# An attention block's output product: sums of weight blocks and the residual made by transfers in DRAM, a fixed order, and three of seven products one after another

## The chip, the cores and the metric

One core of one Trainium2 chip runs one program. The metric is the device time of one execution in microseconds. TensorE (PE in the rows) does the matrix products, VectorE (DVE) and ScalarE (ACT) the elementwise work, GpSimd (POOL) a few masks and casts. Transfers are issued from the queue of SyncE (SP) and from that of GpSimd; 16 DMA engines carry them all.

## The reference

With 512 tokens of width 4096 the reference computes one attention layer and a last RMSNorm:

```python
h = rms_norm(x, norm_g)
proj = h @ w_in + b_in                          # 4096 x 9216: q 4096, k 512, v 512, z 4096
q, k, v, z = jnp.split(proj, [...], axis=-1)
# 64 query heads of 64, 8 key heads; window of 128 keys; one sink a head
p = e / (jnp.sum(e, axis=-1, keepdims=True) + jnp.exp(sink - m))
o = jnp.einsum('bnkgqs,bnskd->bnqkgd', p, vv)
x = x + (o * jax.nn.silu(z)) @ w_out + b_out    # 4096 x 4096
return rms_norm(x, final_g)
```

All is float32. The kernel keeps that precision by splitting each operand of a product into a rounded half "hi" and the rest "lo", and by three TensorE passes for each block: hi·hi, hi·lo, lo·hi.

## The kernel before

**First part, until about 1744 us.** The value columns are multiplied first, then 68 tiles of 128 columns of `w_in` (a key tile for every two key groups, four q tiles and four z tiles for each of eight groups). A tile takes eight chunks (`kc`) of 12 products. SyncE loads `raw` (512 KB, two chunks); ScalarE rounds it to `whi`, VectorE subtracts to `wlo`. The steps of the attention are put between the chunks by a clock of chunks (`at`, `tick`): `scores`, then `turn` (transpose, round, and up to four GpSimd masks, L464), two ticks later `attend`. When the four query blocks of a head pair and its gate are there, `finish` multiplies them and GpSimd's queue stores the head pair to `gT` in DRAM (L550). TensorE's instructions keep program order (`mm`, `tr`); the order on the other engines comes from a scheduler.

**Second part, the output product, from there to the end.** Left operand (the gated heads, transposed) and `w_out` are cut into 2 x 2 blocks, and seven products M1 to M7 of sums of blocks (Strassen) take the place of eight. Each has four column chunks (`p`) of 512, each chunk eight steps (`j`), each step 12 matmuls for two row blocks. They run in three stages. `chunk_35` does M3 and M5 side by side, `chunk_167` M1, M6 and M7, `chunk_42` M4 and M2. A step of `chunk_167` loads four blocks of `w_out`, GpSimd's queue adds a fifth to one of them in SBUF by an accumulating transfer (L771), and VectorE adds two pairs (L681). Then each right operand is rounded by ScalarE (L146) and subtracted by VectorE (L147) into a ring of four slots (`RING`). The left operands are loaded from `gT` as stages, added by VectorE, and split the same way (`left_35`, `left_167`, `left_42`). The residual `x` is loaded into the four output tiles `y` early in `chunk_35` (`begin`, 1 MB each) and `b_out` is added there by accumulating transfers.

At the end of each chunk the accumulators are added into `y` all together:

```python
    for i in range(2):
        a, b = y_of(i, p * CW, CW), y_of(2 + i, D // 2 + p * CW, CW)
        add(a, m1[i], a)
        add(b, m1[i], b)
```

The left operands of the first three quarters of M3 and M5 are made while the last tile of the first part runs (`FIRST`). The last chunk of `chunk_42` scales the rows and stores them.

Of the kernel before, what the change touches and what calls it, by code (L numbers as in the profile page):

```python
# [35 lines left out]
LATE = NP // 2  # L36
EPS = 1e-5
# [5 lines left out]
LAST = 3  # L43

# [7 lines left out]
def hybrid_block_kernel(  # L52
# [20 lines left out]
    ps_m = ctx.enter_context(tc.tile_pool(name="ps_m", bufs=4, space=PS))  # L73
    wpool = ctx.enter_context(tc.tile_pool(name="wpool", bufs=1))
    xg = ctx.enter_context(tc.tile_pool(name="xg", bufs=1))
    small = ctx.enter_context(tc.tile_pool(name="small", bufs=1))
# [57 lines left out]
    gT = dram.tile([KT, P, S], F32, name="gT")  # L134
    def block_of(u, v, j):

        kt = (v * NQ + j) * KC
        return gT[kt:kt + KC, :, u * HALF:(u + 1) * HALF].rearrange("k p s -> p k s")
# [40 lines left out]


    def left(n, src):

        t = slot(n, [P, 2, KC, HALF], "left")
        split(src, t[:, 0], t[:, 1])
        return t

    def fetch_blocks(t, *blocks):
        for i, b in enumerate(blocks):
            nc.sync.dma_start(t[:, i], block_of(*b))

    L35 = {}
    staged = {}

    def stage_35(j):
        staged[j] = slot(j % 2, [P, 2, KC, HALF], "stage", F32)
        fetch_blocks(staged[j], (0, 0, j), (0, 1, j))

    def left_35(j):

        t = staged[j]  # L200
        a = left(L_35[j][0], t[:, 0])
        nc.vector.tensor_tensor(t[:, 0], t[:, 0], t[:, 1], op=ALU.add)
        L35[j] = a, left(L_35[j][1], t[:, 0])

    L_35 = ((2, 3), (4, 5), (8, 9), (10, 11))
    RING = (6, 7, 12, 13)
    FIRST = {
        0: lambda: behind(lambda: (stage_35(0), stage_35(1))),
        2: lambda: behind(lambda: left_35(0)),
        3: lambda: behind(lambda: left_35(1)),  # L210
        4: lambda: behind(lambda: stage_35(2)),
        5: lambda: behind(lambda: left_35(2)),
    }


    with ExitStack() as ph:
        att = ph.enter_context(tc.tile_pool(name="att", bufs=1))
# [4 lines left out]
        def split_w(raw, j, copy=nc.scalar.copy):  # L222
            hi = att.tile([P, CW], F32R, name="whi", tag="whi", bufs=WB)
            lo = att.tile([P, CW], F32R, name="wlo", tag="wlo", bufs=WB)
# [323 lines left out]
        def finish(g, p, o, z):  # L548
            nc.vector.tensor_tensor(o, o, z, op=ALU.mult)
            nc.gpsimd.dma_start(gT[g * 4 + p], o)  # L550
# [93 lines left out]
        while due:  # L644
            tick()
# [332 lines left out]
```

## Time and profile before

| what | value |
|---|---|
| time before, median of 3 runs | 2556.26 us (2554.64 to 2563.33) |
| the profiled execution: its time / its span | 2559.72 us / 2557.9 us |
| TensorE busy | 2395.6 us, 94% of the span |
| VectorE busy | 1541.1 us, 60% |
| ScalarE busy | 950.7 us, 37% |
| GpSimd busy | 313.0 us, 12% |
| mean DMA rate | 150 GB/s |
| mean granted clock of TensorE | 0.973 |

The span is the time from the first to the last instruction of the profiled execution; all stretches below are counted from its start. TensorE's busy time includes matmuls that run slowly or overlap, so a busy TensorE isn't a TensorE at its best pace; how many matmuls a stretch holds tells more.

### The profile page before, as it was taken

The numbers are of one execution on the slowest core, as the hardware profiler recorded it, in microseconds if no ns is written. First come the engines' busy times: TensorE is split into PE (matmuls) and PEld (weight loads), VectorE is DVE, ScalarE is ACT, GpSimd is POOL, SyncE is SP. The second block draws the span as 40 slices with busy tenths as digits, with TensorE's granted clock in tenths as the row PEclk, the third lists the DMA queues.
The fourth block names the chain that finished last, engine by engine and source line by source line (L and its number), as shares of the span: only waits on it lengthen the run. The fifth ranks groups of instructions, "written<-read, shape, count | busy, mean of one in ns | idle before, by whom it ended". The sixth has DMA issues, their size and how long they took to land.

```text
span 2557.9 us, 29388 instructions
## 1 busy us (share of the span) xinstructions
PE 2395.6 (94%) x10604; PEld 1945.4 (76%) x10604; DVE 1541.1 (60%) x2462; ACT 950.7 (37%) x1867; POOL 313.0 (12%) x454
## 2 busy tenths in 40 slices
PE   9999999999999999999999999995699788888986
PEld 7888888888888888888888888874477566666765
DVE  5445655646556555565464655664768666576667
ACT  6433433424333333343333343341334322233434
POOL 1101211201021021021020111111000000000000
PEclk9999999999999999999999999997899999999998
DMA  9523332233232232332333323336777988898555
GB/s 336 177 91 94 90 103 92 90 111 91 91 105 90 88 108 88 99 97 91 99 93 99 99 83 105 97 122 207 248 240 238 284 245 244 242 300 273 181 166 213
DMA packets 119315, 384.24 MB, mean 150 GB/s; under 512 B 12992, under 2 KB 29376, under 8 KB 117376
## 3 DMA queue, kind: packets, MB, share of 16 engines
q1 hardware_dynamic: 104032, 329.37, 39.0%
q0 software_dynamic: 14992, 52.70, 8.6%
q8 instruction: 84, 1.38, 0.2%
q14 instruction: 63, 0.52, 0.1%
q10 hardware_dynamic: 144, 0.28, 0.0%
HBM read 361.32 MB, written 20.97 MB: 149 GB/s over the span
## 4 chain that ended last, share of the span: by engine, by line
PE 70%; DMA 16%; DVE 9%; issue 4%; ACT 1%; SPq 0%; POOL 0%; DVEq 0%; ACTq 0%; POOLq 0%
PE acc L115 65%; DMA raw<-in_w_out 13%; DVE right L147 3%; DMA stage<-gT 2%; DVE raw L681 2%; PE ps L115 2%; PE po L115 2%; DVE y L681 1%; PE pt L118 1%; DMA y<-in_x 1%; ACT right L146 0%; DVE left L147 0%; DMA yd<-st 0%; DVE stage L681 0%; DVE st L681 0%
## 5 line engine op out<-in xcount | busy, mean ns | idle before, releaser
L115 PE MATMUL acc<-xhi,whi 128*128 128x512 f32 x2176 | 863.3, 397 | 0.0
L115 PE MATMUL acc<-xhi,wlo 128*128 128x512 f32 x2176 | 861.0, 396 | 0.0
L115 PE MATMUL acc<-xlo,whi 128*128 128x512 f32 x2176 | 860.7, 396 | 0.0
L115 PE MATMUL acc<-right,left 128*128 128x512 f32 x2688 | 663.4, 406 | 133.2 <-ACT right L146 67.6
L115 PEld LDWEIGHTS acc<-right,left 128*128 128x128 f32 x2688 | 520.5, 196 | 275.8 <-DVE right L147 87.6
L147 DVE TENSOR_TENSOR wlo<-raw,whi 128x512 fp32r<-128x512 f32 x576 | 402.9, 700 | 527.6 <-ACT whi L146 518.3
L146 ACT CAST whi<-raw 128x512 fp32r<-128x512 f32 x575 | 357.0, 621 | 880.6 <-PE acc L115 833.9
L115 PEld LDWEIGHTS acc<-xhi,wlo 128*128 128x128 f32 x2176 | 411.3, 189 | 94.7
L115 PEld LDWEIGHTS acc<-xhi,whi 128*128 128x128 f32 x2176 | 411.8, 189 | 87.9
L115 PEld LDWEIGHTS acc<-xlo,whi 128*128 128x128 f32 x2176 | 411.4, 189 | 88.0
L146 ACT CAST right<-raw 128x1024 fp32r<-128x1024 f32 x224 | 230.1, 1047 | 435.9 <-DMA raw<-in_w_out 223.0
L147 DVE TENSOR_TENSOR right<-raw,right 128x1024 fp32r<-128x1024 f32 x224 | 268.4, 1218 | 71.9 <-ACT right L146 71.5
L681 DVE TENSOR_TENSOR raw<-raw 128x1024 f32<-128x1024 f32 x128 | 156.2, 1222 | 176.8 <-DMA raw<-in_w_out 169.0
L464 POOL TENSOR_SCALAR_AFFINE_SELECT ww<-wh 64x512 fp32r<-64x512 f32 x64 | 42.5, 664 | 913.6 <-ACT wh L460 913.6
L536 DVE RECIPROCAL e<-e 128x128 f32<-128x128 f32 x128 | 120.4, 942 | 0.4
L438 ACT ACTIVATE prob<-ps,nm 128x128 f32<-128x128 f32 x256 | 90.4, 365 | 74.2 <-DVE nm L429 73.2
L513 ACT COPY ot<-po 64x256 f32<-64x256 f32 x128 | 46.9, 366 | 66.5 <-DVE o L514 39.7
L771 POOL DMA_DIRECT2D raw<-in_w_out x32 | 27.5, 859 | 318.8 <-DVE raw L681 172.1
L514 DVE TENSOR_TENSOR o<-po,ot 64x256 f32<-64x256 f32 x128 | 52.8, 412 | 20.9 <-ACT ot L513 20.3
L313 DVE TENSOR_TENSOR tmp<-acc,rbc 128x512 f32<-128x512 f32 x37 | 25.6, 692 | 66.0 <-PE acc L115 66.0
L387 DVE SCALAR_TENSOR_TENSOR q<-tmp,bcol,q 64x512 fp32r<-64x512 f32 x64 | 58.7, 917 | 7.3 <-ACT q L386 6.3
L447 DVE TENSOR_SCALAR prob<-prob,den 128x128 f32<-128x128 f32 x256 | 56.0, 282 | 2.2
(130 smaller groups left out, 1606.5 us busy)
## 6 DMA issues: line engine op xcount, KB each, us to landing
raw<-in_w_in SPq DMA_DIRECT2D x272, 512.0 KB, 3.6
raw<-in_w_out SPq DMA_DIRECT2D x256, 512.0 KB, 5.5
stage<-gT SPq DMA_DIRECT2D x32, 512.0 KB, 6.5
raw<-in_w_out POOLq DMA_DIRECT2D x32, 512.0 KB, 8.7
row<-in_x POOLq DMA_DIRECT2D x16, 512.0 KB, 6.0
gT<-o POOLq DMA_DIRECT2D x32, 256.0 KB, 2.3
xraw<-in_xT SPq DMA_DIRECT2D x15, 512.0 KB, 6.7
raw<-in_w_v SPq DMA_DIRECT2D x15, 512.0 KB, 6.2
```

Of the source, the lines that this page charges most:

```text
L115: tc.keep_in_program_order(nc.tensor.matmul(*a, **k))
L146: copy(hi, src),
L147: nc.vector.tensor_tensor(lo, src, hi.bitcast(F32), op=ALU.subtract),
L387: nc.vector.scalar_tensor_tensor(q2[other, :, h, :], tv[own], b[own], q2[own, :, h, :].bitcast(F32), op0=ALU.add, op1=ALU.subtract,)
L438: nc.scalar.activation(pr[:, u, a, :], ps[:, u, a, 0:P], AF.Exp, bias=nm[:, u, a:a + 1], scale=SCALE, accum_out=den[:, u, a:a + 1],)
L447: nc.vector.tensor_scalar_mul(pr[:, u, a, :], pr[:, u, a, :], den[:, u, a:a + 1])
L464: nc.gpsimd.affine_select(out=out, in_=src.bitcast(F32), fill=0.0, pattern=[[0, 8], [1 if own else -1, QH]], compare_op=ALU.is_ge if own e ...
L513: nc.scalar.copy(ot[own], pq[other, :, :, h, :])
L514: nc.vector.tensor_tensor(ov[own], pq[own, :, :, h, :], ot[own], op=ALU.add)
L536: nc.vector.reciprocal(c, c)
L681: nc.vector.tensor_tensor(out, a, b, op=op)
L771: nc.gpsimd.dma_start(r21, part_w(1, 1, p, j), accum_op=ALU.add)
```

## The change

It has five parts.

1. **Sums of `w_out` in DRAM.** `sums_in_dram` lists 96 pairs of blocks (the right operands of M1, M6 and M7) and 32 pieces of `x` with `b_out`. `make_sums`, called at every second chunk of the first part, issues from GpSimd's queue either a copy of one block into DRAM or, four copies later, a transfer that adds the second block to it there. Each is made to wait for ScalarE's rounding of the weight chunk at hand.
2. **Sums of left blocks in DRAM.** `keep_g` stores each head pair to `gT` in another layout, and by three more transfers into `left_sum` (for M5, M1 and M2); for the later half of the heads those three accumulate.
3. **One product at a time.** `chunk_167` becomes `chunk_single`, called for M1, M6 and M7 in turn: a step loads one sum, splits it and runs 12 matmuls.
4. **Fixed order.** In the second part SyncE's loads, ScalarE's and VectorE's work keep program order (`q`, `ordered`), except in the last chunk. What is to be done at a chunk's end is put in a queue (`later`), and a step of the next chunk takes one item of it (`some`).
5. **Residual.** `y` is first written by copies of the accumulators, and the pieces of `xb` are added to it by accumulating transfers, or loaded where they are first needed. The SBUF pools are laid out anew (`small` first, `halves` apart).

The diff, cut to its core:

```diff
+    gT = dram.tile([2, 2 * NQ, P, KC, HALF], F32, name="gT")
+    left_sum = {m: dram.tile([NQ, P, KC, HALF], F32, name=f"left{m}") for m in (5, 1, 2)}
+    right_sum = {m: dram.tile([NH2, NP, P, 2 * CW], F32, name=f"right{m}") for m in (1, 6, 7)}
+    xb = dram.tile([NB, P, D], F32, name="xb")
+
+    def part_w(u, v, p, j):
+
+        return w_out[NH2 * v + p, NP * u + j]
+
+    def sums_in_dram():
+        for p in range(NH2):
+            for j in range(NP):
+                for m, a, b in ((1, (0, 0), (1, 1)), (6, (0, 0), (0, 1)), (7, (1, 0), (1, 1))):
+                    yield right_sum[m][p, j], part_w(*a, p, j), part_w(*b, p, j)
+            for c in range(2):
+                cs = slice((2 * p + c) * CW, (2 * p + c + 1) * CW)
+                for tb in range(NB):
+                    yield xb[tb][:, cs], x[tb * P:(tb + 1) * P, cs], b_out[:, cs].broadcast_to([P, CW])
+
+    def keep_g(g, p, o):
+
+        nc.gpsimd.dma_start(
+            gT[:, g, :, p].rearrange("u q s -> q u s"), o.rearrange("q (u s) -> q u s", u=2)
+        )
+        late = g >= NQ
+        for m, u in ((5, 0), (1, int(late)), (2, 1)):
+            out, half = left_sum[m][g % NQ][:, p], o[:, u * HALF:(u + 1) * HALF]
+            if late:
+                nc.gpsimd.dma_start(out, half, accum_op=ALU.add)
+            else:
+                nc.gpsimd.dma_start(out, half)
...
+    def right_35(p, j):
+        r12, r22 = raw_w(part_w(0, 1, p, j)), raw_w(part_w(1, 1, p, j))
+        add(r12, r12, r22, ALU.subtract)
+        w5 = right(r22)
+        return right(r12), w5
...
+        def make_sums():
+            do = next(sums_to_do, None) if len(begun) < AHEAD else None
+            if do:
+                out_, a, b = do
+                begun.append((out_, b))
+                turn_ = nc.gpsimd.dma_start(out_, a, max_dma_last_dim=4 * CW)
+            elif begun:
+                out_, b = begun.pop(0)
+                turn_ = nc.gpsimd.dma_start(out_, b, accum_op=ALU.add, max_dma_last_dim=4 * CW)
+            else:
+                return
+
+            tc.add_manual_dep(
+                turn_.ins, latest[1].ins.name,
+                mybir.DependencyInfo(mybir.DependencyClass.Sync, mybir.DependencyReason.DATA),
+                reason="pace",
+            )
...
-                if t == NT - 1 and kc in FIRST:
-                    FIRST[kc]()
+                if t == NT - 1 and kc == 0:
+                    behind(lambda: (stage_35(0), stage_35(1)))
+                if t == NT - 1 and kc == 2:
+                    behind(lambda: left_35(0))
+                if t == NT - 1 and kc == NC - 1:
+                    behind(lambda: first.append(right_35(0, 0)))
+                if t and kc % 2:
+                    make_sums()
...
+    def left_of(m, j, n):
+        if m == 1 or m == 2:
+            t = staging(left_sum[m][j])
+        elif m == 4:
+            t = staging(gT[1, NQ + j])
+        else:
+            v = 0 if m == 6 else NQ
+            t, b = (staging(gT[u, v + j]) for u in ((1, 0) if m == 6 else (0, 1)))
+            add(t, t, b, ALU.subtract)
+        L[m, j] = left(n, t)
...
+    def some():
+        if queue:
+            queue.pop(0)()
...
+        def land(i):
+            a, b = chunk_of(i, p), chunk_of(2 + i, NH2 + p)
+            q(nc.scalar.copy(b, m3[i]))
+            q(nc.scalar.mul(a, m5[i], -1.0))
+            add(sts[i], m3[i], sts[i])
+            add(sts[i], m5[i], sts[i])
+            residual(a, i, p, accum_op=ALU.add)
+            residual(b, 2 + i, NH2 + p, accum_op=ALU.add)
...
+    def chunk_single(m, p, between):
+        acc = accumulator()
         for j in range(NP):
+            w = right(raw_w(right_sum[m][p, j]))
+            if j in between:
+                between[j]()
+            if j > 2:
+                some()
+            mm_pair(acc, m, j, w)
...
-            r11, r22, r12, r21 = (raw_w(u, v, p, j) for u, v in ((0, 0), (1, 1), (0, 1), (1, 0)))
-            nc.gpsimd.dma_start(r21, part_w(1, 1, p, j), accum_op=ALU.add)
-            add(r22, r22, r11)
-            w1 = right(r22)
-            add(r12, r12, r11)
-            w6, w7 = right(r12), right(r21)
...
+    ordered[0] = True
+
+    for p in range(NH2):
+        between = {
+            0: {0: lambda: left_35(1), 2: lambda: (stage_35(2), left_35(2)),
+                4: lambda: (stage_35(3), left_35(3))},
+            1: {k: lambda k=k: left_of(1, k // 2, (14, 15, 0, 1)[k // 2]) for k in (0, 2, 4, 6)},
+        }
+        chunk_35(p, between.get(p, {}))
+    for p in range(NH2):
+        chunk_single(1, p, {
+            1: lambda: left_of(6, p, (2, 3, 4, 5)[p]),
+            5: lambda: left_of(7, p, (8, 9, 10, 11)[p]),
+        })
+    for p in range(NH2):
+        chunk_single(6, p, {1: lambda: left_of(4, p, (14, 15, 0, 1)[p])} if p < 2 else {})
+    for p in range(NH2):
+        chunk_single(7, p, {
+            1: lambda: left_of(2, p, (2, 3, 4, 5)[p]),
+            5: lambda: left_of(4, p, (14, 15, 0, 1)[p]) if p > 1 else None,
+        })
+    for i in range(2):
+        for n, (tb, h) in ((8 + i, (i, 1)), (10 + i, (2 + i, 0))):
+            y[tb, h] = slot(n, [P, D // 2], f"y{tb}{h}", F32)
+    for p in range(NH2):
         chunk_42(p)
```

**Where instructions move: GpSimd in the first part.** Below, its rows after the third `turn` of a head quad, before the change; `qq` is a cast for the next quad, `gT` the store of a head pair.

```order
L464 AFFINE_SELECT ww<-wh 64x512
L464 AFFINE_SELECT ww<-wl 64x512
L464 AFFINE_SELECT wh<-wh 64x512
L464 AFFINE_SELECT wl<-wl 64x512
L550 DMA gT<-o 128x512 x2
L397 CAST qq<-q_1969 64x8x64 x2
```

And the rows there after it; `right_94` and `right_95` are the sums for M6 and M7, `left_90` to `left_92` those for M5, M1 and M2. L621 is a copy, L624 an accumulate.

```order
L524 AFFINE_SELECT ww<-wh 64x512
L524 AFFINE_SELECT ww<-wl 64x512
L524 AFFINE_SELECT wh<-wh 64x512
L524 AFFINE_SELECT wl<-wl 64x512
L621 DMA right_94<-in_w_out 256x512
L164 DMA gT<-o 128x2x256
L173 DMA left_90<-o 128x256
L173 DMA left_91<-o 128x256
L173 DMA left_92<-o 128x256
L624 DMA right_94<-in_w_out 256x512
L621 DMA right_95<-in_w_out 256x512
```

Transfers for the sums now stand before and after the masks, and each store of a head pair has become four.

**VectorE in the last tile of the first part.** Before, ahead of `prob`, the row that TensorE's last transposes wait for:

```order
L539 SCALAR_TENSOR_TENSOR z<-z,bcol,e 128x512
L514 TENSOR_TENSOR o<-po,ot 64x2x2x64
L147 TENSOR_TENSOR left<-stage,left 128x1024
L433 TENSOR_TENSOR es<-nm,sink 128x4
L514 TENSOR_TENSOR o<-po,ot 64x2x2x64
L147 TENSOR_TENSOR left<-stage,left 128x1024
L443 TENSOR_TENSOR den<-den,es 128x4
L202 TENSOR_TENSOR stage<-stage 128x1024
L444 RECIPROCAL den<-den 128x4
L681 TENSOR_TENSOR raw<-raw 128x1024
L447 TENSOR_SCALAR prob<-prob,den 128x128 x4
```

The same place after it:

```order
L599 SCALAR_TENSOR_TENSOR z<-z,bcol,e 128x512
L239 TENSOR_TENSOR right<-raw,right 128x1024
L574 TENSOR_TENSOR o<-po,ot 64x2x2x64
L493 TENSOR_TENSOR es<-nm,sink 128x4
L574 TENSOR_TENSOR o<-po,ot 64x2x2x64
L503 TENSOR_TENSOR den<-den,es 128x4
L504 RECIPROCAL den<-den 128x4
L507 TENSOR_SCALAR prob<-prob,den 128x128 x4
```

The left operands of the second and third quarter, their additions and one weight addition no longer stand there.

**SyncE's queue at the start of the second part.** Before (`y_14618` to `y_14627` are the four output tiles):

```order
L668 DMA raw<-in_w_out 128x1024 x2
L700 DMA y_14618<-in_x 128x2048
L700 DMA y_14621<-in_x 128x2048
L700 DMA y_14624<-in_x 128x2048
L700 DMA y_14627<-in_x 128x2048
L700 DMA st<-in_x 128x512 x2
L755 DMA stage<-gT 128x4x256
L668 DMA raw<-in_w_out 128x1024
```

After:

```order
L228 DMA raw<-in_w_out 128x1024 x5
L228 DMA stage<-gT 128x1024
L228 DMA stage<-left_90 128x1024
L228 DMA raw<-in_w_out 128x1024 x4
L228 DMA stage<-gT 128x1024
L228 DMA stage<-left_90 128x1024
L228 DMA raw<-in_w_out 128x1024 x4
L228 DMA st<-xb 128x512 x2
```

The four 1 MB loads of `x` are gone from between the weights; only weights, stages and two pieces of `xb` follow one another.

## Rows read from the trace of the kernel before

**Rows 1.** By stretch: us, busy (count) PE PEld DVE ACT POOL, clock, DMA share, GB/s.
```profile
100.00:1700.00 1600.00, 1600.00 (x7365) 1320.40 (x7364) 911.67 (x1749) 591.42 (x1402) 237.44 (x341) 1.00 0.31 97
...
1744.00:1811.00 67.00, 25.55 (x99) 19.64 (x98) 27.01 (x29) 13.82 (x15) 7.34 (x10) 0.70 0.88 269
1811.00:1960.00 149.00, 138.16 (x586) 110.48 (x586) 112.64 (x115) 58.69 (x65) 10.32 (x15) 0.99 0.69 224
1960.00:2312.00 352.00, 293.38 (x1156) 225.46 (x1154) 228.93 (x214) 108.90 (x111) 28.36 (x34) 0.94 0.88 264
2312.00:2500.00 188.00, 167.91 (x696) 133.57 (x696) 132.59 (x139) 72.89 (x93) 4.79 (x7) 0.95 0.64 203
```

**Rows 2.** Busy time in a stretch with few stalls.
```profile
1900.00:1950.00 50.00, 47.22 (x206) 38.13 (x205) 36.09 (x37) 20.84 (x24) 4.55 (x7) 1.00 0.68 221
```

**Rows 3.** The groups of the output product's instructions by line.
```profile
L115 PE MATMUL acc<-right,left 128*128 128x512 f32 x2688 | 663.4, 406 | 133.2 <-ACT right L146 67.6 <-DVE right L147 63.1 <-DVE sq L852 2.2
...
L147 DVE TENSOR_TENSOR right<-raw,right 128x1024 fp32r<-128x1024 f32 x224 | 268.4, 1218 | 71.9 <-ACT right L146 71.5
L146 ACT CAST right<-raw 128x1024 fp32r<-128x1024 f32 x224 | 230.1, 1047 | 435.9 <-DMA raw<-in_w_out 223.0 <-PE acc L115 139.7 <-DVE raw L681 70.1
L681 DVE TENSOR_TENSOR raw<-raw 128x1024 f32<-128x1024 f32 x128 | 156.2, 1222 | 176.8 <-DMA raw<-in_w_out 169.0 <-issue 7.4
```

**Rows 4.** TensorE's waits from 1960 to 2312 us: total, times, longest.
```profile
PE acc L115 <- DVE right L147: 38.2, 32, 4.5
PE acc L115 <- ACT right L146: 20.2, 13, 4.3
```

**Rows 5.** DMA queues from 1960 to 2312 us: packets, MB, share of 16 engines.
```profile
q1 hardware_dynamic: 25423, 75.51, 60.8%
q0 software_dynamic: 4824, 17.09, 26.6%
```

**Rows 6.** TensorE's timeline at the start of the second part: start, us, instruction.
```profile
1743.87 5.65 PE L115 MATMUL acc<-right,left 128*128 128x512 f32 x24
...
1763.59 18.16 PE L115 MATMUL acc<-right,left 128*128 128x512 f32 x71 [1.65 <-DVE right L147]
1808.43 0.80 PE L115 MATMUL acc<-right,left 128*128 128x512 f32 x1 [26.69 <-ACT right L146]
```

**Rows 7.** GpSimd's and SyncE's timelines there.
```profile
1751.68 0.55 POOL L550 DMA_DIRECT2D gT<-o  x1 [0.83 <-DVE o L549]
...
1754.33 0.34 SPq L668 DMA_DIRECT2D raw<-in_w_out  x1
...
1756.35 2.29 SPq L700 DMA_DIRECT2D y<-in_x  x4
```

**Rows 8.** VectorE's groups from 1700 to 1744 us.
```profile
L147 DVE TENSOR_TENSOR left<-stage,left 128x1024 fp32r<-128x1024 f32 x7 | 8.4, 1213 | 2.8 <-ACT left L146 2.8
L202 DVE TENSOR_TENSOR stage<-stage 128x1024 f32<-128x1024 f32 x3 | 3.8, 1256 | 0.0
```

**Rows 9.** The tail: TensorE's last row in its timeline.
```profile
2502.16 38.23 PE L115 MATMUL acc<-right,left 128*128 128x512 f32 x155 [2.98 <-DVE right L147]
```

**Rows 10.** DMA from 100 to 1700 us: two queues, and a weight load's time to landing.
```profile
q1 hardware_dynamic: 38705, 140.96, 28.6%
q0 software_dynamic: 4015, 12.51, 2.3%
...
raw<-in_w_in SPq DMA_DIRECT2D x267, 512.0 KB, 3.6
```

**Rows 11.** GpSimd's issues by line.
```profile
L771 POOL DMA_DIRECT2D raw<-in_w_out x32 | 27.5, 859 | 318.8 <-DVE raw L681 172.1 <-DMA raw<-in_w_out 73.2 <-DVE y L681 22.5
...
L550 POOL DMA_DIRECT2D gT<-o x32 | 17.6, 550 | 179.9 <-DVE o L549 179.9
```

**Rows 12.** A head block's last mask and the product that needs it, in the timeline.
```profile
1307.44 1.17 POOL L464 TENSOR_SCALAR_AFFINE_SELECT wl<-wl 64x512 fp32r<-64x512 f32 x1
...
1308.95 0.28 PE L115 MATMUL po<-wh,vv 128*128 128x256 f32 x1
```

More of the change, by code (lines that the diff above doesn't have):

```diff
@@ L177, in load_w, with q, take @@
         return raw
-    def left(n, src):
[L183 to L191, printed above, removed]
+    ordered = [False]
+    def q(ins):
+        return tc.keep_in_program_order(ins) if ordered[0] else ins
+    RING = (6, 7, 12, 13)
+    count = {"raw": 0, "acc": 0, "w": 0}
+    def take(name):
+        count[name] += 1
+        return count[name] - 1
@@ new lines, in load, with raw_w, divide, right @@
+    def load(t, src):
+        q(nc.sync.dma_start(t, src))
+    def raw_w(src):
+        pool = outp if take("raw") // RAW % 2 else wpool
+        raw = pool.tile([P, 2, CW], F32, name="raw", tag="raw", bufs=RAW)
+        load(raw, src.rearrange("p (j c) -> p j c", j=2))
+        return raw
+    def divide(src, t):
+        q(nc.scalar.copy(t[:, 0], src))
+        q(nc.vector.tensor_tensor(t[:, 1], src, t[:, 0].bitcast(F32), op=ALU.subtract))
+        return t
+    def right(raw, place=None):
+        t = slot(RING[take("w") % 4] if place is None else place, [P, 2, 2, CW], "right")
+        return divide(raw, t)
@@ L192, in hybrid_block_kernel, with add @@
+    def left(n, src):
+        return divide(src, slot(n, [P, 2, KC, HALF], "left"))
+    def add(out, a, b, op=ALU.add):
+        q(nc.vector.tensor_tensor(out, a, b, op=op))
+    def right_35(p, j):
[3 more added lines that the diff above has]
+        return right(r12), w5
+    first = []
+    L = {}
     staged = {}
     def stage_35(j):
-        staged[j] = slot(j % 2, [P, 2, KC, HALF], "stage", F32)
@@ L196, in stage_35 @@
-        fetch_blocks(staged[j], (0, 0, j), (0, 1, j))
+        staged[j] = t = slot(j % 2, [P, 2, KC, HALF], "stage", F32)
+        load(t[:, 0], gT[0, j])
+        load(t[:, 1], left_sum[5][j])
     def left_35(j):
[L200 to L213, printed above, removed]
+        n = ((2, 3), (4, 5), (8, 9), (10, 11))[j]
@@ L643, in hybrid_block_kernel @@
                 evacuate(g_, name, acc)
+        assert not begun and next(sums_to_do, None) is None
         while due:
@@ L691, in mm_pair, with mm_block @@
-    def mm_pair(acc, j, lt, rt):
-        for i in range(2):
-            mm_block(acc[i], i, j, lt, rt)
+            (ps_m, ps_n)[take("acc") // 4 % 2].tile([P, CW], F32, name="acc") for _ in range(2)
+        ]
+    def mm_block(acc, i, m, j, rt):
+        for k in range(2):
+            l = L[m, j // 2][:, :, (2 * j + k) % KC, i * P:(i + 1) * P]
+            mm(acc[i], l[:, 0], rt[:, 0, k], start=(j == k == 0), stop=False)
+            mm(acc[i], l[:, 0], rt[:, 1, k], start=False, stop=False)
+            mm(acc[i], l[:, 1], rt[:, 0, k], start=False, stop=(j == NP - 1 and k == 1))
@@ L703, in gains_of, with chunk_of, residual @@
+    def chunk_of(tb, cc):
+        return y_of(tb, cc * CW, CW)
+    def residual(t, tb, cc, **k):
+        src = xb[tb][:, cc * CW:(cc + 1) * CW]
+        if k:
+            nc.gpsimd.dma_start(t, src, **k)
+        else:
+            load(t, src)
     def gains_of(cc):
@@ L811, in chunk_42 @@
             w4 = right(r21)
-            late = last and j >= LATE
-            w2 = right(r11, (S_42[0] + S_42[1])[j - LATE] if late else None)
-            mm_pair(m4, j, L42[j // 2][0], w4)
+            if j > 1:
+                some()
+            if j == (1 if last else NP - 2):
+                fgs = [gains_of(p), gains_of(NH2 + p)]
+                for i in range(2):
+                    residual(chunk_of(2 + i, p), 2 + i, p)
+                    load(chunk_of(i, NH2 + p), yd[i][:, cs])
```

226 lines of the change are left out of this document (86 added, 140 removed).

## The prediction

> **What bounds the kernel now.** I read the busy time by stretch first, with its count of matmuls. Until 1700 us TensorE is busy throughout, VectorE for 57%, GpSimd for 15%, and the DMA engines at 0.31 [rows 1]. The part after that is where time is lost. The output product has 2688 matmuls [rows 3]. In a stretch with few stalls 206 of them fill 47.22 us, so one takes 0.2292 us [rows 2] and all of them 616 us. They are spread from 1743.87 [rows 6] to 2502.16 + 38.23 = 2540.39 us [rows 9], over 796.5 us: 180 us are lost. By stretch [rows 1], length less 0.2292 a matmul: 44 us from 1744 to 1811 (99), 15 to 1960 (586), 87 to 2312 (1156), 29 to 2500 (696), and 5 after that.
>
> The reader should then see the cause of each. The 87 us belong to M1, M6 and M7 side by side. TensorE waits there for right operands, 38.2 and 20.2 us and more that is hidden in slow matmuls [rows 4], under a DMA share of 0.88. SyncE's queue moved 75.51 MB in 0.608 of 352 us, 2.83 us a MB; GpSimd's, which there is nearly all accumulates, 17.09 MB in 0.266, or 5.48 us a MB [rows 5]. A step needs four loads of 0.524 MB and one accumulate: 5.9 + 2.9 = 8.8 us of DMA, against 36 matmuls or 8.25 us. VectorE's five passes (1.222 and 1.218 us each [rows 3]) make 6.1 us. So the DMA binds, and that before any stage load. The 44 us are a wait for weights behind the heads' last store, then one of 26.69 us [rows 6] while 4 MB of `x` stand in SyncE's queue ahead of a stage [rows 7].
>
> **The change part by part.**
>
> *Middle stage.* A step of one product needs one load, 0.524 MB: at 3.25 us a MB (140.96 MB in 0.286 of 1600 us [rows 10]) 1.7 us, against 12 matmuls or 2.75 us. VectorE needs 1.2 us, ScalarE 1.05 [rows 3]. In M1's chunks four stage loads join eight weights: 6.3 MB, 20.4 us against 22.0, the tightest place. TensorE becomes the bound, and the 87 us go.
>
> *Stages with two products.* A step keeps one addition and two subtractions, 3.66 us of VectorE against 5.50. The first chunk adds three pairs of left operands, 7.3 us: 36.6 of 44. What changes is that additions at a chunk's end no longer stand in one block ahead of the next right operands.
>
> *What stays of stalls there.* No row shows the new order. One end is none. The other is the share lost from 1811 to 1960, 15 of 149 us [rows 1], over the remaining 611 us: 60 us. I take a third, 20 us: work at chunk ends is spread, but M1's chunks are close to the DMA's pace.
>
> *Last tile of the first part.* Five of the seven left subtractions and three stage additions leave VectorE there, 6.1 + 3.8 = 9.9 us [rows 8]. One subtraction of 1.2 us comes earlier, so `prob` and with it the last matmul come 8.7 us earlier. Ends: 0, if another wait takes the place, and 12.7, with the 2.8 us of waiting in the same row.
>
> *The gap after it.* Before, TensorE runs 24 matmuls at 1743.87 and resumes for good at 1763.59 [rows 6]: the last head pair is stored from 1751.68, weights are loaded from 1754.33 [rows 7]. That chain stays, since the new buffers lie on memory of the first part. It gets six more issues on GpSimd's queue, three a head pair, at 0.55 to 0.86 us [rows 11]: 3.3 to 5.2; I take 4.5. So it resumes at 1763.59 - 8.7 + 4.5 = 1759.4 us. The loads of `x` behind it are gone from the queue; what takes their place, two pieces of `xb` and accumulates into `y` a chunk later, has a stage's time to land.
>
> *Sums in the first part.* 96 copies and 96 accumulates of 0.524 MB, 32 of each of half that: 58.7 MB twice. At 3.25 us a MB for copies and 5.48 for accumulates: 191 + 322 us of all DMA engines. The heads' 96 more transfers, 12.6 MB, half of them accumulates, add 53 at 2.94 (12.51 MB in 0.023 of 1600 [rows 10]) and 5.48. That is 566 us in 1600, so the share goes from 0.31 to 0.66. No row has an accumulate whose target is DRAM. Bounds: copies at the accumulates' price and accumulates at twice theirs give 1037 us, a share of 0.96. I take the nearer end. Weight loads, which land in 3.6 us [rows 10], have two more buffers behind them of 5.5 us each, so I cost the first part at nothing. The cover is gone when a load takes more than about 11 us.
>
> *GpSimd's queue.* 352 more issues, about 248 us by rows 11 (128 and 48 of each price; all at one price: 194 to 303): busy 15% to 30%. Behind an issue stand the masks that `attend` needs. In one head block of each of the 16 quads the last mask ends only 0.34 us before its product [rows 12]; that one comes a chunk after the nearest paced issue, the others have more room. I cost this at nothing, with 16 x (0.86 - 0.34) = 8 us as the end above.
>
> *A rule against it.* The rows show GpSimd's issues at 0.55 and 0.86 us beside a VectorE that is busy 57% of the time [rows 1, 11]. The Trainium skill, "SBUF — State Buffer", section "Summary: rules for kernel authors", says that descriptors made by GpSimd starve while VectorE runs its fast modes, and to issue such transfers from SyncE or ScalarE. By that rule each of the 352 issues could wait for a VectorE instruction, and this would be the second rival below. The rows show no such stretching so far.
>
> *Sum.* 1759.4 + 2664 x 0.2292 = 610.6, and 1.9 for the lower clock at the start (71 matmuls in 18.16 us [rows 6] against 16.3; granted 0.70 in that stretch [rows 1]) gives 2371.9. Stalls 20, and the tail as before, 2557.9 - 2540.4 = 17.5: a span of 2409.4. The profiled execution lies 1.8 us above its span and 0.14% above the median of the runs: 2411.2, which answers to **2408 us**, 5.8% less. A change of 0.3% is about what a measurement here can tell.
>
> **The rivals.**
>
> *Stalls stay.* The fixed order makes VectorE and SyncE wait for a late item with ready ones behind it, and 60 us are lost instead of 20: 2448. For it: even the stretch of rows 2 loses 2.8 of 50 us. Against it: VectorE's load falls from five passes a step to one in the middle.
>
> *GpSimd is late.* Issues, their waits for older transfers or stretched descriptors delay the masks; TensorE runs in program order and waits at `attend`. If each of the 48 head blocks that mask four times comes 2 us late beyond its slack, 96 us are lost: 2504. Against it: masks of two of three such blocks have more than 0.34 us of room.
>
> *The middle stage isn't bound by DMA.* Then its 87 us stay in another wait: 2495. Against it: 8.8 us of DMA a step against 8.25.
>
> *Slower: the DMA engines fill up in the first part.* Accumulates into DRAM must read and write there. If one costs so much that the weight loads fall behind, every us beyond the 1104 that are free (0.69 of 1600) lengthens the first part. To lose the whole gain of some 150 us, 1104 + 150 less the copies (191 + 19) must go to 65 MB of accumulates: 16 us a MB, three times the row's price. At four times, 65 x 21.9 + 210 = 1634 us, the time is 2408 + 530 = 2938. For it: no row excludes it. Against it: the nearest row is three times lower.
>
> **How the numbers follow.** The forecast 0.65, stalls that stay 0.14, a late GpSimd 0.10, another bound in the middle 0.04, full DMA engines 0.06, no effect for other reasons 0.01. The first has its own range of 2378 to 2430 (no stalls and 1759 three us earlier; or 35 us of stalls and 8 for GpSimd). The range to 2460 adds the stalls that stay, with GpSimd's 8 us and some more: 0.80. Faster: all but the last two and part of the last but one, 0.92; same 0.02; slower 0.06.
>
> **What would show it.** Until 1700 us TensorE as busy as before with about 7365 matmuls and the DMA share near 0.66 show the sums hidden; waits of TensorE for GpSimd would show the second rival, a share near 1 and weight loads over 11 us the last. The output product should resume near 1759 us. M1, M6 and M7, 1152 matmuls, should take about 264 us plus a few, at a granted clock near 1. If waits for right operands pass 30 us over the second part, the 20 us are wrong.

## The result and the profile after

The changed kernel takes **2357.11 us** (median of 4 runs, 2356.63 to 2357.83) against 2559.8 us (2554.64 to 2564.37) for the kernel before: a ratio of 0.9209, interval 0.9187 to 0.9231. The forecast was 2408 us with a range from 2375 to 2460. The direction was right; the time lies 18 us under the range.

First the busy time by stretch of the changed kernel, with the columns of [rows 1]:

```profile
100.00:1700.00 1600.00, 1598.27 (x7494) 1337.41 (x7493) 938.58 (x1794) 605.76 (x1436) 509.65 (x699) 1.00 0.69 179
...
1900.00:1950.00 50.00, 50.00 (x222) 41.42 (x221) 40.52 (x42) 25.13 (x30) 4.63 (x7) 1.00 0.96 344
1960.00:2312.00 352.00, 352.00 (x1554) 291.47 (x1554) 239.88 (x237) 154.92 (x171) 2.16 (x4) 1.00 0.66 223
```

From 1960 to 2312 us 1554 matmuls run without a gap, where 1156 ran in [rows 1]. And until 1700 us there are 7494 instead of 7365, though TensorE was busy all the time before as well, at the same granted clock of 1.00. That is the surprise of this case.

TensorE's waits from 1700 us to the end (total, times, longest); [rows 4] had 58.4 us in 352 us alone:

```profile
PE acc L117 <- ACT right L238: 20.3, 3, 17.2
PE acc L117 <- DVE right L239: 2.3, 4, 0.8
```

TensorE's timeline from the first matmuls of the output product, which answers to [rows 6, 9]:

```profile
1699.90 5.63 PE L117 MATMUL acc<-right,left 128*128 128x512 f32 x24
1722.72 0.79 PE L117 MATMUL acc<-right,left 128*128 128x512 f32 x1 [17.19 <-ACT right L238]
1724.06 166.74 PE L117 MATMUL acc<-right,left 128*128 128x512 f32 x720 [0.55 <-DVE right L239]
1890.99 421.67 PE L117 MATMUL acc<-right,left 128*128 128x512 f32 x1859 [0.19 <-DVE right L239]
...
2321.14 17.76 PE L117 MATMUL acc<-right,left 128*128 128x512 f32 x71 [0.82 <-DVE right L239]
```

One wait is left that matters, at the seam between the parts. After it TensorE works almost without a break to 2338.90 us.

The DMA queues from 100 to 1700 us, as in [rows 10], and the loads and sums there with their time to landing:

```profile
q0 software_dynamic: 59341, 141.33, 41.9%
q1 hardware_dynamic: 39555, 144.01, 27.1%
...
raw<-in_w_in SPq DMA_DIRECT2D x267, 512.0 KB, 4.8
right<-in_w_out POOLq DMA_DIRECT2D x192, 512.0 KB, 6.4
```

GpSimd's issues of the sums by line, which answer to [rows 11]; L624 accumulates, L621 copies:

```profile
L624 POOL DMA_DIRECT2D right<-in_w_out x96 | 92.9, 967 | 302.3 <-ACT whi L181 297.1 <-ACT wh L520 4.6 <-issue 0.6
L621 POOL DMA_DIRECT2D right<-in_w_out x96 | 56.3, 586 | 313.9 <-ACT whi L181 296.1 <-issue 12.2 <-PE po L117 5.5
```

**Where the forecast and the profile part.** The forecast's span was 2409.4 us; the profiled one is 2355.8, or 53.6 less. The first part ends at 1699.90 instead of 1735.2 (35.3 us). The gap from there to 1724.06 is 24.2 us, as forecast. From 1724.06 to TensorE's last matmul it takes 614.8 us instead of 632.5 (17.7). The tail is 16.9 instead of 17.5 (0.6).

Most of the 35.3 us are in the matmuls of the first part. The chain of waits of the kernel before has runs of 216 of them (start, us, engine, tile):

```profile
213.54 50.40 PE acc L115 x216
```

That is 0.2333 us a matmul. The same run after the change, 0.2268:

```profile
210.12 48.99 PE acc L117 x216
```

The timeline of the kernel before shows the quick pace too, in the output product, between two waits:

```profile
1899.67 11.04 PE L115 MATMUL acc<-right,left 128*128 128x512 f32 x48
1911.49 23.87 PE L115 MATMUL acc<-right,left 128*128 128x512 f32 x104 [0.78 <-DVE right L147]
```

The 48 matmuls start over 11.04 - 0.39 us (0.39 is what one takes to its end), so 47 steps of 0.2266 us. Matmuls of one size, 128 x 512, so had two paces in the kernel before, 0.2333 in the first part and 0.2266 in the second, and the difference is in no wait that the profile names.

### The profile page after: what moved, and what is told of

Its sections match the earlier page's. It is cut to its first block, busy times and chain, and to the rows that moved or that the text cites. A ratio compares the mean times of both kernels' runs of the same rounds, so it can differ in the third digit from the quotient of the medians.

```text
span 2355.8 us, 29752 instructions
## 1 busy us (share of the span) xinstructions
PE 2313.2 (98%) x10604; PEld 1923.9 (82%) x10604; DVE 1455.5 (62%) x2370; ACT 962.1 (41%) x1883; POOL 555.6 (24%) x776
## 4 chain that ended last, share of the span: by engine, by line
PE 95%; DVE 2%; DMA 1%; ACT 1%; issue 0%; POOL 0%; SPq 0%; DVEq 0%; ACTq 0%
PE acc L117 90%; PE ps L117 2%; PE po L117 2%; PE pt L120 1%; DVE right L239 1%; DMA raw<-in_w_out 0%; DVE raw L251 0%; DMA left<-o 0%; DVE y L251 0%; DMA stage<-left 0%; PE idle L117 0%; ACT acc L808 0%; DVE e L596 0%; DVE y L981 0%; DMA yd<-st 0%
## 5 line engine op out<-in xcount | busy, mean ns | idle before, releaser
L117 PE MATMUL acc<-xhi,whi 128*128 128x512 f32 x2176 | 849.6, 390 | 0.0
L117 PE MATMUL acc<-xlo,whi 128*128 128x512 f32 x2176 | 848.3, 390 | 0.0
L117 PE MATMUL acc<-xhi,wlo 128*128 128x512 f32 x2176 | 848.1, 390 | 0.0
L117 PE MATMUL acc<-right,left 128*128 128x512 f32 x2688 | 616.4, 391 | 22.6 <-ACT right L238 20.3
L117 PEld LDWEIGHTS acc<-right,left 128*128 128x128 f32 x2688 | 507.2, 189 | 131.5 <-ACT right L238 21.6
L239 DVE TENSOR_TENSOR right<-raw,right 128x1024 fp32r<-128x1024 f32 x224 | 273.3, 1224 | 131.8 <-ACT right L238 130.5
L624 POOL DMA_DIRECT2D right<-in_w_out x96 | 92.9, 967 | 302.3 <-ACT whi L181 297.1
L621 POOL DMA_DIRECT2D right<-in_w_out x96 | 56.3, 586 | 313.9 <-ACT whi L181 296.1
L804 POOL DMA_DIRECT2D fg<-in_final_g x12 | 6.7, 556 | 407.8 <-DVE y L251 402.1
L251 DVE TENSOR_TENSOR raw<-raw 128x1024 f32<-128x1024 f32 x64 | 78.0, 1219 | 30.8 <-DMA raw<-in_w_out 30.8
```

The source lines that it names most:

```text
L117: tc.keep_in_program_order(nc.tensor.matmul(*a, **k))
L239: q(nc.vector.tensor_tensor(t[:, 1], src, t[:, 0].bitcast(F32), op=ALU.subtract))
L251: q(nc.vector.tensor_tensor(out, a, b, op=op))
L621: turn_ = nc.gpsimd.dma_start(out_, a, max_dma_last_dim=4 * CW)
L624: turn_ = nc.gpsimd.dma_start(out_, b, accum_op=ALU.add, max_dma_last_dim=4 * CW)
```

## The experiments

**The pace: is it the transfers and the order, or where tiles lie?** The first theory is that the new place of the pool `small` gave it; the rival is that something else in the change did. `b_small_first` is the kernel before with this one line moved:

```diff
+    small = ctx.enter_context(tc.tile_pool(name="small", bufs=1))
     wpool = ctx.enter_context(tc.tile_pool(name="wpool", bufs=1))
     xg = ctx.enter_context(tc.tile_pool(name="xg", bufs=1))
-    small = ctx.enter_context(tc.tile_pool(name="small", bufs=1))
```

> The kernel before, with one line moved: the pool of small tiles is made ahead of the pools of weights and of x instead of behind them, which moves every tile of those two pools up by 960 bytes in each partition and nothing else. Theory (the pace of the matmuls hangs on where their operands lie in SBUF, and this line alone gave it): matmuls of the attention follow each other every 0.227 us instead of 0.232, those of the output projection every 0.225 instead of 0.229; some 7600 x 0.005 + 2664 x 0.004 = 49 us less, about 2510 us. Rival (the quicker pace of the changed kernel comes from its transfers, its order or the place of the weight halves): no change, 2552 to 2565 us, 216 matmuls still take 50.4 us.

Measured: 2527.58 us (2526.57 to 2527.94), ratio 0.9866 (0.9839 to 0.9892), 216 matmuls in 48.99 us. The whole gain is in the first part, which ends 33.8 us earlier (1710.11 instead of 1743.87). The second part's 11 us did not come: there both operands lie in slots of x, which in each kernel are a multiple of 8192 bytes apart, and the median step from one matmul to the next is 0.227 us in both.

`a_small_back` moves the line back in the changed kernel.

> The changed kernel, with the pool of small tiles back behind the pools of weights and of x. Theory (place in SBUF): the old pace returns in both parts, 2357 + 38 + 11 = about 2406 us, which is the time that was predicted. Rival (transfers and order make the pace): 2355 to 2360 us, 216 matmuls in 49.0 us.

Measured: 2389.16 us (2387.31 to 2391.71). Its chain of waits has the old pace:

```profile
212.94 50.40 PE acc L117 x216
```

and its timeline the end of the first part:

```profile
1730.81 5.60 PE L117 MATMUL acc<-right,left 128*128 128x512 f32 x24
```

So the line alone is worth 1730.81 - 1699.90 = 30.9 us in the changed kernel, all in the first part; the second keeps its pace (1775 matmuls in 402.64 us in its chain, 402.65 in that of the changed kernel).

`b_halves` is the kernel before with only the weight halves in a pool of their own:

```diff
+        halves = ph.enter_context(tc.tile_pool(name="halves", bufs=1))
         att = ph.enter_context(tc.tile_pool(name="att", bufs=1))
-            hi = att.tile([P, CW], F32R, name="whi", tag="whi", bufs=WB)
-            lo = att.tile([P, CW], F32R, name="wlo", tag="wlo", bufs=WB)
+            hi = halves.tile([P, CW], F32R, name="whi", tag="whi", bufs=WB)
+            lo = halves.tile([P, CW], F32R, name="wlo", tag="wlo", bufs=WB)
```

> The kernel before, with the halves of the weights (whi, wlo) in a pool of their own ahead of the attention's pool, as the changed kernel has them; x and the weights' landing tiles stay where they are. Theory (it is the place of x and of the slots that counts): no change, 2550 to 2566 us. Rival (the place of the stationary operand counts): the attention's matmuls get to 0.227 us, about 38 us less, 2520 us; the second part, which doesn't use them, keeps 0.229 us.

Measured: 2561.35 us, ratio 1.0 (0.9986 to 1.0014), 216 in 50.40 us. That pool by itself did nothing.

**Which property of the place?** A tile of 16, 48 or 80 numbers a partition, put into a pool of the kernel before, moves all that lies behind it. `b_pad64`, and the others with another size or pool:

```diff
+    pad = small.tile([P, 16], F32, name="pad")
+    nc.gpsimd.memset(pad, 0.0)
```

> The kernel before, with 64 bytes of padding behind its pool of small tiles: x and the landing tiles stay where they are (xhi at byte 30848 of a partition, 128 above a multiple of 2048), the weight halves and all else of the attention move up by 64 (whi from 177728 to 177792). Theory A (what counts is how the two operands of a matmul lie to each other: in the quick kernels whi and xhi differ by a multiple of 512 bytes, in the slow ones by 448 more; here it is a multiple of 512 again): the attention's matmuls go to 0.227 us, about 34 us less, 2523 to 2532 us. Theory B (the place of x alone counts): no change, 0.232 us, 2554 to 2567 us.

> The kernel before, with 64 bytes of padding ahead of the pools of weights and x and 64 more behind them: xhi comes to 192 above a multiple of 2048, whi to 1728, so their difference is a multiple of 512, and x lies at 64 above a multiple of 128 as it does in the quick kernels. Theory A (the difference counts) and theory B (the place of x counts) both: 0.227 us, 2523 to 2532 us. If it stays at 0.232 us and 2554 to 2567 us, neither holds as stated, and it is another property of the place.

> The kernel before, with 192 bytes of padding behind its pool of small tiles: x stays at 128 above a multiple of 2048, the weight halves come to 1792; they differ by 128 above a multiple of 512, which is a multiple of 128 but not of 256. If the difference must be a multiple of 128 alone: the attention's matmuls go to 0.227 us, 2524 to 2535 us, as with 64 bytes of padding. If it must be a multiple of 256 or 512: they stay at 0.232 us, 2554 to 2567 us.

> The kernel before, with 320 bytes of padding behind its pool of small tiles: x stays, the weight halves come to a difference of 256 above a multiple of 512 bytes. If the difference must be a multiple of 256: 0.227 us, 2524 to 2535 us. If it must be one of 512: 0.232 us, 2554 to 2570 us.

> The kernel before, with 64 bytes of padding between the landing tiles of the weights and x: x and the weight halves move up by 64, the landing tiles stay. The weight halves and x still differ by 448 above a multiple of 512 bytes; the weight halves and the landing tiles, from which they are made, now differ by a multiple of 512. If the two operands of the matmul must agree: no change, 0.232 us, 2554 to 2570 us. If it is the halves and their landing tiles (that is, ScalarE's and VectorE's work): 0.227 us, 2524 to 2535 us.

> The kernel before, with 64 bytes of padding between the landing tiles of the weights and x, and 64 more behind the pool of small tiles: the weight halves and x differ by a multiple of 512 bytes again, the weight halves and their landing tiles by 128 above one. If the two operands of the matmul must agree and the landing tiles don't count: 0.227 us, 2524 to 2535 us. If the landing tiles must agree as well (which the middle pace of 0.229 us with x alone moved leaves possible): 0.229 us or slower, 2540 to 2565 us.

What they gave, with the bytes as the built programs have them. "whi - xhi" is what the difference of the two operands' places leaves over a multiple of 512, "whi - raw" that of the weight halves and their landing tiles; the matmuls are those from 100 to 900 us by busy time. The kernel before, run again beside each of them, took 2558.74 to 2561.84 us in the median. Several of these rows are medians of two runs, and the two of `b_pad64` lie 15 us apart (2524.22 and 2539.19): read the count of matmuls first, and the time second.

| kernel | whi - xhi | whi - raw | matmuls | time, us |
|---|---|---|---|---|
| before | 448 | 448 | 3688 | 2559.8 |
| b_halves | 448 | 448 | 3688 | 2561.35 |
| b_pad192 | 128 | 128 | 3674 | 2567.12 |
| b_pad_x | 448 | 0 | 3718 | 2544.94 |
| b_small_first | 0 | 0 | 3757 | 2527.58 |
| b_pad64 | 0 | 0 | 3757 | 2531.7 |
| b_pad64_both | 0 | 0 | 3757 | 2533.15 |
| b_pad320 | 256 | 256 | 3757 | 2527.27 |
| b_pad_x_both | 0 | 64 | 3757 | 2524.0 |
| a_small_back | 448 | 448 | 3689 | 2389.16 |
| after | 0 | 0 | 3757 | 2357.11 |

Theory A holds: where the two operands' places differ by a multiple of 256 bytes, the pace is the quick one, wherever x itself lies (128, 192 or, in `b_small_first`, 1088 above a multiple of 2048). The place of the halves alone isn't it either: `whi` starts at byte 177728 in the kernel before and in `b_small_first`, and at 177792 in `b_pad64` and in `b_pad_x`, and each time one is quick and the other not. The 256 rests on one kernel, `b_pad320`; the other quick ones differ by a multiple of 512. A multiple of 128 is not enough (`b_pad192`). The landing tiles don't count: `b_pad_x_both` is quick with halves and landing tiles apart (by 64; the expectation's 128 was a slip), and `b_pad_x` isn't with them alike. But `b_pad_x` is a miss for both theories: it has the difference of the kernel before, x lies 64 bytes further, and its pace lies between, 49.45 us for 216 (0.2289):

```profile
215.32 49.45 PE acc L117 x216
```

So among disagreeing places there are better and worse ones; why is open, and so is what in the chip makes disagreeing places slower.

**The fixed order.** `a_free_order` lets the scheduler order the engines in the second part:

```diff
-        ordered[0] = not last
...
-    ordered[0] = True
+    ordered[0] = False
```

> The changed kernel, with the engines of the output projection free to be put in order by the scheduler, instead of kept in the order in which the code is written. Theory (the fixed order is what ended the 64 us of waits for right operands of the stretch 1960 to 2312): some of the waits come back, 2365 to 2400 us. Rival (the transfers' sums did it, with one load and no addition for a right operand; the order is worth nothing): 2354 to 2361 us.

Measured: 2403.77 us (2402.17 to 2406.15), 46.7 more, a little over the expected bound. TensorE's waits from 1695 us on:

```profile
PE acc L117 <- DVE right L239: 28.3, 23, 6.5
PE acc L117 <- ACT right L238: 18.1, 1, 18.1
PE pt L120 <- DVE prob L507: 4.9, 1, 4.9
```

The third row is at the end of the first part, where work of the second now stands ahead of `prob`; with it TensorE gets through the seam 9.0 us later (1733.07 instead of 1724.06). The second row is the seam itself. The first takes the place of 2.3 us; with it, and at a lower granted clock (0.92 from 1724 to 1811 us and 0.94 to 1960, where the changed kernel has 0.96 and 1.00), the output product takes 650.7 us from there to its last matmul instead of 614.8. The rival falls: with sums from DRAM the order is still worth about 47 us. But it isn't worth them where the theory looked for them: the 744 matmuls of M3 and M5 behind the seam take 201.2 us instead of 173.6, while the 1152 of M1, M6 and M7 take 264.0 instead of 261.1 (361.2 in the kernel before).

**The right operands' sums.** `a_sbuf_sums` makes them on VectorE:

```diff
-            w = right(raw_w(right_sum[m][p, j]))
+            a, b = PARTS[m]
+            r, s = raw_w(part_w(*a, p, j)), raw_w(part_w(*b, p, j))
+            add(r, r, s)
+            w = right(r)
```

> The changed kernel, with the three right operands of M1, M6 and M7 made as sums on VectorE again from two loaded blocks each, instead of being summed by transfers in DRAM beside the attention; the residual and the left operands are as in the changed kernel. Theory (the sums in DRAM take loads out of a stretch that the transfers bound): 96 right operands need 192 loads of 524288 bytes, 100.7 MB, which at the 344 GB/s that this stretch of the changed kernel reached at a share of 0.96 take 293 us and with its other loads some 320 us, where the 1152 matmuls take 261 us: 40 to 80 us more, 2395 to 2440 us, and the first part is no shorter. Rival (loads and additions lie behind the matmuls): 2354 to 2361 us.

Measured: 2494.63 us (2492.44 to 2495.93), 137.5 more, over the expected bound. All of it is in M1, M6 and M7: 398.3 us for their 1152 matmuls instead of 261.1. The stretch from 1900 to 2300 us, the two largest waits there, and three rows of VectorE's timeline:

```profile
1900.00:2300.00 400.00, 313.41 (x1162) 221.45 (x1161) 278.81 (x255) 122.91 (x124) 5.22 (x7) 0.96 0.82 286
...
ACT right L237 <- DVE raw L250: 258.7, 96, 3.7
DVE right L238 <- ACT right L237: 112.0, 94, 1.2
...
2002.89 1.22 DVE L250 TENSOR_TENSOR raw<-raw 128x1024 f32<-128x1024 f32 x1
2005.30 1.23 DVE L238 TENSOR_TENSOR right<-raw,right 128x1024 fp32r<-128x1024 f32 x1 [1.19 <-ACT right L237]
2006.44 1.22 DVE L250 TENSOR_TENSOR raw<-raw 128x1024 f32<-128x1024 f32 x1
```

The theory had the wrong cause. The stretch moved 286 GB/s, not the 344 that I had taken from a stretch of 50 us, and at 286 the 100.7 MB alone would take 352 us; but the DMA engines were not full (0.82), and neither ScalarE nor VectorE waited for a load there. VectorE was the bound: it adds, stands 1.19 us while ScalarE rounds, subtracts, and in the fixed order only then adds for the next step. That is 3.55 us from addition to addition, beside 2.72 us for 12 matmuls, and VectorE's other additions come on top: it is busy for 278.81 us and waits for ScalarE for 112.0, together 391 of 400. So the run shows what the sums in DRAM are worth in this order; what the second load of each operand costs by itself no run shows. The first part, without these sums, still has 216 matmuls in 48.99 us and ends in the same gap, after which TensorE resumes at 1724.49 (1724.06 with them): the sums cost nothing there.

**How much room is in the first part?** `a_sums_twice` makes each right sum a second time, for nobody:

```diff
+                    yield twin[m][p, j], part_w(*a, p, j), part_w(*b, p, j)
...
-                if t and kc % 2:
+                if t:
                     make_sums()
```

> The changed kernel, with each sum of right operands made a second time into DRAM that nothing reads, so that 192 more transfers of 524288 bytes go beside the attention. The DMA share there, 0.69 with 179 GB/s, would become about 1.0 with 305 GB/s. Theory (the sums cost nothing as long as the attention's weights come in before they are needed, and that ends when the engines are full): weights land later than the 10.8 us that three landing tiles allow, TensorE starts to wait for them, 2380 to 2550 us. Rival (still hidden): 2354 to 2361 us.

Measured: 2359.22 us (2357.4 to 2361.05). From 100 to 900 us:

```profile
100.00:900.00 800.00, 800.00 (x3756) 669.75 (x3755) 469.80 (x897) 303.02 (x720) 348.54 (x491) 1.00 1.01 270
```

and the weights' landing there:

```profile
raw<-in_w_in SPq DMA_DIRECT2D x136, 512.0 KB, 6.8
```

The engines are full by their share (1.01) and move 270 GB/s instead of 182, weights land in 6.8 us, and TensorE runs as many matmuls as before. The rival holds: still hidden. The bound of 10.8 us was not reached, so where the cover ends isn't shown.

**One product at a time.** `a_side` puts M1, M6 and M7 side by side again:

```diff
-        acc = accumulator()
+        accs = {m: accumulator() for m in (1, 6, 7)}
         for j in range(NP):
-            w = right(raw_w(right_sum[m][p, j]))
+            ws = {m: right(raw_w(right_sum[m][p, j])) for m in accs}
...
-            mm_pair(acc, m, j, w)
+            for m in accs:
+                mm_pair(accs[m], m, j, ws[m])
```

> The changed kernel, with M1, M6 and M7 of a chunk side by side again (three right operands for each block, six accumulators, the landing additions of a chunk ahead of the next one's matmuls), with the sums still from DRAM and the order still fixed. Theory (one by one, a chunk has two accumulators, so its landing lies beside the next chunk's matmuls): side by side some 5 us of additions in each of four chunks stand ahead of matmuls, 2365 to 2385 us. Rival (with sums from DRAM the order of the products is worth nothing): 2354 to 2361 us.

Measured: 2382.39 us (2380.8 to 2383.23), 25.3 more: the size fits, the place doesn't. The waits are not at each chunk's landing but in the last chunk of M3 and M5 and the one after it. Its timeline:

```profile
1871.97 0.49 PE L117 MATMUL acc<-right,left 128*128 128x512 f32 x1 [2.27 <-ACT right L238]
1874.98 13.13 PE L117 MATMUL acc<-right,left 128*128 128x512 f32 x47 [2.51 <-DVE right L239]
...
1909.27 0.50 PE L117 MATMUL acc<-right,left 128*128 128x512 f32 x1 [4.10 <-ACT right L238]
...
1936.32 399.92 PE L117 MATMUL acc<-right,left 128*128 128x512 f32 x1763 [0.95 <-DVE right L239]
```

After 1936.32 us 1763 matmuls follow without a named wait. M1, M6 and M7 themselves take 263.6 us side by side, 261.1 one after another; M3 and M5 take 194.3 instead of 173.6. These rows suggest that what one product at a time saves is the crowding of the left operands of M6 and M7, which side by side fall due within one chunk; no run tests that by itself.

**The gap at the seam.** `a_raw_low` only asks for the `y` tiles later, so that the landing tiles of the second part come to lie over the weight halves:

```diff
+        if p == 0:
+            for i in range(2):
+                for tb, h in ((2 + i, 1), (i, 0)):
+                    y[tb, h] = outp.tile([P, D // 2], F32, name=f"y{tb}{h}", tag="y", bufs=4)
```

> The changed kernel, with the y tiles of the output projection asked for only when they are first written, so that its own landing tiles for weights come to lie over the weight halves of the first part instead of over the attention's tiles. Theory (TensorE's 24 us at the seam wait for weights whose landing place is the attention's last o tile, which is still being sent to DRAM): the load starts when the last weight halves are used up, and the gap goes from 24 to 8 to 14 us, 2341 to 2349 us. Rival (the gap waits for the sums of attention outputs themselves): no change, 2355 to 2359 us.

Measured: 2357.75 us (2357.16 to 2358.41): no change. SyncE issues these loads at 1718.12 us (1717.97 in the changed kernel), after the attention's last transfer, whatever lies beneath. That fits loads that wait for the end of the first part's pools as a whole. `a_seam` therefore takes four landing tiles from slots of x:

```diff
+    EARLY = (3, 4, 5, 9)
...
+        if n in EARLY:
+            at_ = EARLY.index(n)
+            if at_ % 2 == 0:
+                spare[0] = slot(14 + at_ // 2, [P, 2, 2, CW], "spare", F32)
+            raw = spare[0][:, at_ % 2]
+        else:
+            pool = outp if n // RAW % 2 else wpool
+            raw = pool.tile([P, 2, CW], F32, name="raw", tag="raw", bufs=RAW)
```

> The changed kernel, with four of the first landing tiles for weights of the output projection (the loads numbered 3, 4, 5 and 9) put into two slots of x that are idle there, since the pool that has them otherwise waits for the whole of the attention's pools to end. Theory (the 17 us wait at the seam is the wait of that pool): the gap from the first 24 matmuls to the rest shrinks from 24 us to 10 to 16 us, as VectorE still has the last reciprocals and the second left operand to do ahead of the right operands; 2342 to 2350 us. Rival (another wait, for the left operands' sums in DRAM, takes its place): 2354 to 2360 us.

Measured: **2345.93 us** (2342.81 to 2346.62), 11.2 less than the changed kernel and the best of all; ratio 0.9161 (0.9144 to 0.9178) to the kernel before. Its timeline:

```profile
1699.66 5.86 PE L117 MATMUL acc<-right,left 128*128 128x512 f32 x25
1711.77 48.60 PE L117 MATMUL acc<-right,left 128*128 128x512 f32 x207 [6.25 <-DVE right L249]
```

The gap is 12.1 us instead of 24.2, as the theory said.

## Why the prediction missed

**The step that failed: the first part as busy as before, "with about 7365 matmuls".** The argument looked for what could slow TensorE there and had no term for its pace: the pools' new layout stood in the change and was put at nothing without a reason. It was worth 30.9 us (`a_small_back` against the changed kernel), the largest part of the 53.6. With the one line put back the changed kernel takes 2389.16 us, inside the range: it is this step that took the time out of it.

**Mis-sized: matmuls at 0.2292 us and 20 us of stalls.** The 0.2292 of [rows 2] holds short waits. The pace is 0.2268 (1859 in 421.67), 6.4 us less over 2664. With 2664 at that pace (604.2) and the 1.9 us for the clock at the start, 614.8 leaves 8.7 us of stalls instead of 20, 11.3 less. The rival "stalls stay" had the sign wrong: the fixed order, which was to hold up ready work behind late items, gains 47 us.

**Last tile of the first part: right in kind, 4.4 us too small.** With the old layout it ends at 1730.81, 13.1 us earlier than in [rows 6], where 8.7 was taken and 12.7 was the end. TensorE's wait for `prob` fell from 7.6 to 1.3 us, that for GpSimd's `wh` from 2.6 to 1.6. The sum had no term for the granted clock, which was 0.86 there before (1680 to 1743 us) and is 1.00 (1680 to 1730 us with the old layout).

**The gap: right in size, by two errors that cancel.** It is 24.2 us, 4.4 more than before, where 4.5 was forecast. GpSimd's and SyncE's timelines there:

```profile
1707.10 2.69 POOL L171 DMA_DIRECT2D left<-o  x3
...
1709.50 3.73 POOL L171 DMA_DIRECT2D left<-o  x3
...
1717.97 1.28 SPq L228 DMA_DIRECT2D raw<-in_w_out  x3
```

The loads start 18.1 us after the first of the 24 matmuls, where it was 10.5 [rows 6, 7]: 7.6 more, as the six issues take 2.69 + 3.73 us instead of 4.5 and the loads follow the landing of the last one, at 1717.66. From the loads to TensorE's return it is 6.1 us instead of 9.3, for which there was no term. The size was luck. And the loads don't wait for the memory beneath them, as I had put it: moving them changed nothing (`a_raw_low`), and memory that no closing pool owns freed them (`a_seam`).

**Sums in the first part: right.** A share of 0.69 where 0.66 was worked out; landing in 4.8 us; no cost, and none at twice the traffic. (The upper bound of 1037 us comes to 1069 by its own prices, a share of 0.98; nothing hangs on it.) The rival of full DMA engines is refuted with them: in `a_sums_twice` they were full from 100 to 900 us, and the weights still came in time.

**GpSimd: right.** Its busy time from 100 to 1700 us is 509.65 us (32%; 30% was worked out), and TensorE waited for it for 1.7 us in all (`po` behind `wh` 1.5, behind `wl` 0.2). The issues of the right sums took 586 and 967 ns, near the 550 and 859 of [rows 11], beside a VectorE busy 59% of the time; those of the left sums that accumulate took 1271 ns (L171), and why is open. By the Trainium skill, "SBUF — State Buffer", section "Summary: rules for kernel authors", they could have starved while VectorE ran its fast modes. TensorE's 1.7 us of waits show no such cost here; whether VectorE ran in those modes the trace doesn't show.

**Middle stage: right.** The 87 us went: the 1152 matmuls take 261.1 us where about 264 was forecast. The sums in DRAM carry that. Without them 137.5 us come back (`a_sbuf_sums`), though through VectorE and not, as in the argument, through the DMA engines; without the fixed order, or with the three products side by side, the stage stays within 3 us. What the order and one product at a time gain lies mostly in M3 and M5, where the prediction gave them no price of their own.

## What to carry to other kernels

Before costing an edit, divide the time of a run of matmuls without waits by its count, in each part of the kernel: two paces for one shape at one granted clock are time that no wait shows, and here a pool moved by one line recovered it. Loads that belong beside a long compute part can be hidden there as long as they land within the buffers' depth, even at a DMA share near 1, and a tight stage is relieved by the loads and additions that it no longer makes. At a seam between two sets of pools, let the first loads of the new part land in memory that no closing pool owns.

## What the runs showed of the hardware

The pace of a 128 x 512 matmul hung on how its two operands lie to each other in SBUF: 0.2268 us where their places agree modulo 256 bytes, 0.2324 and 0.2333 where they differ by 128 and 448 above a multiple of 512, and 0.2289 in one place with 448, at a granted clock of 1.00 each time. These are the paces of the long runs; from 100 to 900 us as a whole the place is worth 1.8% more matmuls (3757 in the changed kernel, 3689 in `a_small_back`). In the kernel before, from 500 to 700 us, the matmuls that start while VectorE is idle follow each other every 0.2327 us in the mean, those beside its subtraction for `wlo` every 0.2325: that work beside them is not it. The Trainium skill, "SBUF — State Buffer", section "SBUF: two separate sides", says that TensorE never waits on anyone there. With VectorE's subtraction beside it the pace here was no slower, which agrees. But its own two operands cost it 2.9% in the long runs when they lie badly (0.2333 against 0.2268).

A transfer that accumulates into DRAM, which no row before the change had, took 0.97 us to issue, and the sums (copies and accumulates of 512 KB together) landed in 6.4 us. GpSimd's queue spent 0.419 x 1600 us of all DMA engines on 141.33 MB, 4.7 us a MB, within the bounds of 3.25 and 5.48 that were taken for copies and accumulates.
